# SSD core of a two-block model: the step of a state and what it gives to the next chunk as two steps of the written order

## The chip, the cores and the metric

The kernel runs on one core of a Trainium2 chip. The time is the device time of one execution in microseconds (us). Three runs of the kernel before gave 1649.72, 1649.62 and 1646.17 us, with a median of 1649.62 us.

## The reference

The program computes two blocks of a model on 512 tokens of width 1024. The first block has attention and an SSD mixer side by side and an MLP; the second has an RG-LRU layer and an MLA layer. The change lies in the SSD mixer alone, which works on 4 chunks of 128 tokens, forwards and backwards:

```python
def ssd_chunked(xdt, a, bm, cm):
    ...
    CB = jnp.einsum("bclgn,bcsgn->bgcls", Cc, Bc)
    M = CB[:, :, None] * jnp.exp(segsum(A))
    y_diag = jnp.einsum("bgrcls,bcsgrp->bclgrp", M, X)
    decay_states = jnp.exp(A_cs[..., -1:] - A_cs)
    states = jnp.einsum("bclgn,bgrcl,bclgrp->cbgrpn", Bc, decay_states, X)
    chunk_decay = jnp.moveaxis(jnp.exp(A_cs[..., -1]), -1, 0)
    ...
    def step(hs, inp):
        st, dec = inp
        return dec[..., None, None] * hs + st, hs
    ...
    _, prev = lax.scan(step, h0, (states, chunk_decay))
    y_off = jnp.einsum("bclgn,cbgrpn,bgrcl->bclgrp", Cc, prev, jnp.exp(A_cs))
    return (y_diag + y_off).reshape(b, s, h, p)
```

There are 4 groups of 8 heads. For each group a state is carried over the chunks in either direction, and what a chunk gets from the state of the chunk ahead of it is `y_off`. The inputs of this stage are an in-projection followed by a centred convolution of width 5 (x, B and C) and a gate z; behind it a product with `w_ssd_out` adds to the output.

## The kernel before

Large products are made of three: the activations are kept as a high and a low part (hi and lo), the weights too, and `hi*w_hi`, `lo*w_hi`, `hi*w_lo` are added up in PSUM (lines 174, 175 and 176). A block of one such product takes 24 matmuls of 128x512 here. A weight tile is loaded by a DMA of SP's queue into `wr`, cast to the high part `wh` on ScalarE (L162), and the low part `wl` is `wr - wh` (L165), in this stage on GpSimd (POOL) for two tiles of three and on VectorE (DVE) for the third. `wr`, `wh` and `wl` have four buffers each, so the cast of one weight tile waits until TensorE (PE) has done the last matmul with the `wh` four tiles earlier.

`ssd()` (L677) runs the 4 groups in turn. For each, the generator `ssd_core(g)` (L553) goes through the steps that are written in the string `CORE` (L41):

- **S n**, `state(n)`, n = 0 to 7, even numbers forwards and odd ones backwards, two for each chunk step (only 0 to 5 are needed): `xw` = x times decays on DVE (L596), a matmul with B into a PSUM tile (L598), and the state `st`: a copy on ScalarE for the first of either direction (L601), else `prev * decay` on DVE (L603) and the addition of the PSUM tile on DVE (L604). Then, in the same step, the matmul with C that gives the next chunk's share (L608), and its scaling into `yoff` on DVE (L615, or L612 and L613 where that chunk has been written by the other direction already).
- **M n**, `mixer(n)`, one of the 8 heads: two PE products that spread the cumulated decays (L623), for four chunks `e` (L629 ACT, L631 DVE) and `w` (L633 ACT, L635 DVE), the exponential (L642 ACT) and `e * w` on POOL (L643).
- **Y j**, `output(j)`, two heads each: 4 transposes of `yoff` (L650) and 8 matmuls with the `e` of the two heads (L653), the gate on DVE (L657, L659), a square on ACT (L665) that POOL adds up (L666), and the hi and lo part of the result (L669 ACT, L670 DVE).

Between the steps PE gets other blocks of 24 matmuls, called fills: the previous group's output product, the next group's x, B and C blocks with their convolution (`xbc`; x0 to x3 for x, x4 for B and x5 for C), and this group's gates (`z`, z0 to z3). When a fill is issued goes by its number and by NC (L42): after step number `step` all fills n with `n * NC <= (step + 1) * len(fill)` (L713). In the last group the fills are output products, gates and two steps of the attention's `qkv`.

A scheduler orders the instructions of each engine behind that by the times that it reckons with, so an engine's order is near to the written one but not the same. Each engine runs its instructions in its order: one that waits holds up all behind it.

Of the kernel before, what the change touches and what calls it, by code (L numbers as in the profile page):

```python
# [37 lines left out]
QG = 4  # L38
POM = 0
AORD = "s0 s1 s2 s3 f0 t0 m0 t1 m1 t2 m2 t3 m3 f1".split()  # L40
CORE = "S0 S1 M0 S2 S3 M1 S4 S5 M2 M3 Y0 M4 M5 Y1 M6 M7 Y2 Y3"  # L41
NC = 19  # L42
MODS = [0, 0, 6, 10]
WP = 0
TP = 0
# [14 lines left out]
class Build:  # L60
# [492 lines left out]
    def ssd_core(self, g):  # L553
# [20 lines left out]
        for i in range(2):  # L574
            x = self.t("cb", shape=(128, 4, 128))
# [4 lines left out]
        def hb(ap):  # L580
            return ap.unsqueeze(2).to_broadcast([128, 8, 64])

        def v8(ap):
            return ap.rearrange("p (h d) -> p h d", h=8)

        seen = set()
        prev = {}
        Ms = {}
        out = self.ssdT[g] = []

        def state(n):
            d = n % 2
            c = n // 2 if d == 0 else 3 - n // 2
            xw = self.t("xw")
            o = 32 * d + g * 8
            nc.vector.tensor_tensor(out=v8(xw), in0=v8(xtm[:, c]), in1=hb(self.tk2[:, c, o:o + 8]), op=ALU.mult)  # L596
            p = self.ps()
            nc.tensor.matmul(p, lhsT=Btm[:, c], rhs=xw, start=True, stop=True)  # L598
            st = self.t("st")
            if n < 2:  # L600
                nc.scalar.copy(out=st, in_=p)  # L601
            else:
                self.e("st").tensor_tensor(out=v8(st), in0=v8(prev[d]), in1=hb(self.dcy[:, c, o:o + 8]), op=ALU.mult)  # L603
                nc.vector.tensor_tensor(out=st, in0=st, in1=p, op=ALU.add)  # L604
            prev[d] = st
            cc = c + 1 if d == 0 else c - 1
            p = self.ps()
            nc.tensor.matmul(p, lhsT=CT[:, cc * 128:cc * 128 + 128], rhs=st, start=True, stop=True)  # L608
            eo = hb(self.tk2[:, cc, 64 + o:64 + o + 8])
            if cc in seen:  # L610
                y = self.t("yo")
                nc.vector.tensor_tensor(out=v8(y), in0=v8(p), in1=eo, op=ALU.mult)  # L612
                self.e("yo").tensor_tensor(out=yoff[:, cc], in0=yoff[:, cc], in1=y, op=ALU.add)  # L613
            else:
                nc.vector.tensor_tensor(out=v8(yoff[:, cc]), in0=v8(p), in1=eo, op=ALU.mult)  # L615
                seen.add(cc)
# [54 lines left out]
            out.append((hi, lo))  # L671

        for x in CORE.split():
            {"S": state, "M": mixer, "Y": output}[x[0]](int(x[1:]))
            yield

    def ssd(self, first):  # L677
# [19 lines left out]
        for g in range(4):  # L697
# [14 lines left out]
            for step, _ in enumerate(self.ssd_core(g)):  # L712
                while n < len(fill) and n * NC <= (step + 1) * len(fill):  # L713
                    with self.fills():
# [809 lines left out]
```

## Time and profile before

| | us |
|---|---|
| median of three runs | 1649.62 |
| profiled execution, device time | 1649.19 |
| its span, from the first to the last instruction | 1647.4 |
| PE busy in the span | 1580.8 |
| DVE busy | 1128.2 |
| ACT busy | 789.3 |
| POOL busy | 446.0 |
| the four groups of the SSD core, from us 100 to us 505 of the span | 405.00 |

The span is 1.8 us shorter than the execution's own time. The median of the runs is 0.4 us above that time. The stage that the change touches lies between us 100 and us 505: group 0 up to us 177, group 1 up to us 290, group 2 up to us 402, and group 3 behind it. The three later groups carry more fills than the first.

A line of the trace's timeline has the start in us, the length in us, the engine, the line of the kernel, and what is written and read; in square brackets stands how long the engine had been idle before, and what ended that. Consecutive matmuls overlap: the record of one is longer than the step to the next.

### The profile page before, as it was taken

To read this page: it belongs to the slowest core of one execution; us is meant where nothing else is said; L and a number is where in the kernel's file an instruction comes from. 1 tells how busy PE (TensorE), PEld (TensorE's weight loads), DVE (VectorE), ACT (ScalarE), POOL (GpSimd) and SP (SyncE) were. 2 spreads that over 40 slices of the span, in tenths; PEclk is the share of its full clock that TensorE was granted. 3 is DMA by queue.
4 is the path that set the end of the run, shared out by engine and by line. 5 is a ranking of instruction groups with operands and counts; after the bars stand their busy time and mean duration, and the time that the engine had idled before them with its cause. 6 is when DMAs were issued, how large, how long until landed. Compare 5 with 4: busy or idle time off the path is not lost.

```text
span 1647.4 us, 20884 instructions
## 1 busy us (share of the span) xinstructions
PE 1580.8 (96%) x7696; PEld 1279.2 (78%) x7696; DVE 1128.2 (68%) x1948; ACT 789.3 (48%) x1517; POOL 446.0 (27%) x322
## 2 busy tenths in 40 slices
PE   5989999999999999999999999999999999999998
PEld 3767667677688778778888888888888778988886
DVE  7899679689868988874445343443467884747883
ACT  4356546354465667663334232232336662454652
POOL 3314335244252443431133011111141011321012
PEclk8999999999999999999999999999999999999999
DMA  7612124224222222315313333323323222322211
GB/s 254 196 52 65 52 77 128 75 72 139 91 82 80 80 62 80 96 52 183 111 52 117 101 97 95 102 90 102 105 77 99 87 90 67 100 69 69 65 63 52
DMA packets 50649, 153.54 MB, mean 93 GB/s; under 512 B 8178, under 2 KB 12914, under 8 KB 50547
## 3 DMA queue, kind: packets, MB, share of 16 engines
q1 hardware_dynamic: 50546, 152.22, 28.9%
q8 instruction: 60, 0.98, 0.3%
q14 instruction: 43, 0.34, 0.1%
HBM read 150.10 MB, written 2.10 MB: 92 GB/s over the span
## 4 chain that ended last, share of the span: by engine, by line
PE 67%; DVE 18%; ACT 4%; issue 3%; POOL 3%; DMA 1%; DVEq 0%; POOLq 0%; ACTq 0%
PE pm L175 18%; PE pm L174 18%; PE pm L176 18%; DVE acc L507 3%; DVE wl L165 1%; DVE nmax L752 1%; PE px L608 1%; PE px L848 1%; DVE w L635 1%; PE px L598 1%; DMA wada<-in_w_ada 1%; POOL rs L254 1%; PE px L857 1%; POOL wl L165 1%; PE px L856 1%
## 5 line engine op out<-in xcount | busy, mean ns | idle before, releaser
L162 ACT CAST wh<-wr 128x1024 fp32r<-128x1024 f32 (+5 forms) x245 | 239.7, 980 | 389.3 <-PE pm L175 168.9
L165 DVE TENSOR_TENSOR wl<-wr,wh 128x1024 fp32r<-128x1024 f32 (+2 forms) x170 | 203.3, 1196 | 184.8 <-ACT wh L162 183.9
L165 POOL TENSOR_TENSOR wl<-wr,wh 128x1024 fp32r<-128x1024 f32 (+3 forms) x75 | 174.7, 2330 | 532.9 <-ACT wh L162 486.6
L174 PE MATMUL pm<-hh,wh 128*128 128x512 f32 x432 | 173.8, 406 | 8.2 <-ACT hh L169 6.6
L175 PE MATMUL pm<-hl,wh 128*128 128x512 f32 x432 | 176.0, 407 | 3.9 <-POOL hl L170 3.8
L176 PE MATMUL pm<-hh,wl 128*128 128x512 f32 x432 | 172.9, 401 | 0.0
L983 POOL TENSOR_TENSOR r<-r 128x512 f32<-128x512 f32 x32 | 50.8, 1589 | 252.3 <-ACT r L982 252.3
L174 PE MATMUL pm<-h,wh 128*128 128x512 f32 (+1 forms) x288 | 105.4, 366 | 0.0
L175 PE MATMUL pm<-h,wh 128*128 128x512 f32 (+1 forms) x288 | 105.3, 365 | 0.0
L176 PE MATMUL pm<-h,wl 128*128 128x512 f32 (+1 forms) x288 | 105.2, 365 | 0.0
L174 PEld LDWEIGHTS pm<-hh,wh 128*128 128x128 f32 x432 | 81.8, 190 | 29.9 <-ACT hh L169 8.4
L175 PEld LDWEIGHTS pm<-hl,wh 128*128 128x128 f32 x432 | 82.3, 190 | 27.1 <-POOL hl L170 7.6
L174 PE MATMUL pm<-wh,rh 128*128 128x512 f32 x256 | 99.8, 390 | 0.0
L760 POOL TENSOR_SCALAR pr<-pr,psum 128x512 f32<-128x512 f32 x64 | 64.8, 1024 | 128.8 <-DVE psum L756 71.6
L176 PE MATMUL pm<-wh,rl 128*128 128x512 f32 x256 | 99.6, 389 | 0.0
L175 PE MATMUL pm<-wl,rh 128*128 128x512 f32 x256 | 99.6, 389 | 0.0
L176 PEld LDWEIGHTS pm<-hh,wl 128*128 128x128 f32 x432 | 82.4, 191 | 19.9 <-issue 3.1
L507 DVE SCALAR_TENSOR_TENSOR acc<-pm,conv_w_s,acc 128x510 f32<-128x510 f32 (+2 forms) x118 | 87.4, 741 | 8.3 <-ACT acc L498 7.3
L279 DVE SCALAR_TENSOR_TENSOR wada<-wada,cs 128x1024 f32<-128x1024 f32 x48 | 68.9, 1446 | 16.4 <-DMA wada<-in_w_ada 15.8
L643 POOL TENSOR_TENSOR e<-e,w 128x512 f32<-128x512 f32 x32 | 52.0, 1626 | 101.1 <-ACT e L642 87.0
L755 ACT ACTIVATE pr<-px,nmax 128x512 f32<-128x512 f32 (+2 forms) x96 | 60.5, 638 | 29.8 <-DVE nmax L752 23.9
L174 PE MATMUL pm<-ha,wh 128*128 128x512 f32 (+1 forms) x192 | 68.2, 355 | 0.0
(401 smaller groups left out, 4120.3 us busy)
## 6 DMA issues: line engine op xcount, KB each, us to landing
wr<-in_w_mlp SPq DMA_DIRECT2D x64, 512.0 KB, 3.5
wada<-in_w_ada SPq DMA_DIRECT2D x48, 512.0 KB, 4.0
wr<-in_w_xbc SPq DMA_DIRECT2D x24, 512.0 KB, 3.5
wr<-in_w_in_a SPq DMA_DIRECT2D x20, 512.0 KB, 3.5
wr<-in_w_z SPq DMA_DIRECT2D x16, 512.0 KB, 3.6
wr<-in_w_ssd_out SPq DMA_DIRECT2D x16, 512.0 KB, 3.6
wr<-in_w_gate SPq DMA_DIRECT2D x16, 512.0 KB, 3.7
wr<-in_w_qkv SPq DMA_DIRECT2D x16, 384.0 KB, 3.0
```

The source lines that it names most:

```text
L162: nc.scalar.copy(out=hi[:, :n], in_=raw[:, :n])
L165: eng.tensor_tensor(out=lo[:, :n], in0=raw[:, :n], in1=r32(hi[:, :n]), op=ALU.subtract)
L174: m(out, lhsT=lh, rhs=rh, start=start, stop=False)
L175: m(out, lhsT=lh, rhs=rl, start=False, stop=False)
L176: m(out, lhsT=ll, rhs=rh, start=False, stop=stop)
L254: g.tensor_tensor(out=r, in0=r, in1=self.mhalf.to_broadcast(list(ss.shape)) if len(ss.shape) == 2 else self.mhalf.unsqueeze(2).to_broadcas ...
L279: nc.vector.scalar_tensor_tensor(out=w, in0=w, scalar=1.0, in1=self.cs, op0=ALU.mult, op1=ALU.mult, accum_out=self.modc[:, j:j + 1])
L507: nc.vector.scalar_tensor_tensor(out=acc[:, lo:hi], in0=ps[:, lo + o:hi + o], scalar=w[:, j:j + 1], in1=acc[:, lo:hi], op0=ALU.mult, op1=A ...
L643: self.e("ew").tensor_tensor(out=e, in0=e, in1=w, op=ALU.mult)
L755: nc.scalar.activation(out=e[:, :n], in_=p, func=AF.Exp, bias=nmax, accum_out=s)
L760: self.e("norm").tensor_scalar(out=e[:, :n], in0=e[:, :n], scalar1=s, scalar2=1.0, op0=ALU.mult, op1=ALU.mult)
L983: self.e("sq").tensor_tensor(out=r, in0=r, in1=r, op=ALU.mult)
```

## The change

The step of a state is cut behind the state itself: `state(n)` ends with `st` and puts it into `held`, and a new step **C n**, `carry(n)`, takes it from there, does the matmul with C and scales the result into `yoff`. The string `CORE` places the six new steps, one step or more behind their states, and the number of steps NC by which the fills are spread goes from 19 to 25. The computation is the same.

```diff
--- before.py
+++ after.py
@@ -38,8 +38,8 @@
 QG = 4
 POM = 0
 AORD = "s0 s1 s2 s3 f0 t0 m0 t1 m1 t2 m2 t3 m3 f1".split()
-CORE = "S0 S1 M0 S2 S3 M1 S4 S5 M2 M3 Y0 M4 M5 Y1 M6 M7 Y2 Y3"
-NC = 19
+CORE = "S0 S1 C0 M0 C1 S2 S3 M1 C2 C3 S4 S5 M2 C4 C5 M3 Y0 M4 M5 Y1 M6 M7 Y2 Y3"
+NC = 25
 MODS = [0, 0, 6, 10]
 WP = 0
 TP = 0
@@ -584,7 +584,7 @@
             return ap.rearrange("p (h d) -> p h d", h=8)
 
         seen = set()
-        prev = {}
+        prev, held = {}, {}
         Ms = {}
         out = self.ssdT[g] = []
 
@@ -603,6 +603,14 @@
                 self.e("st").tensor_tensor(out=v8(st), in0=v8(prev[d]), in1=hb(self.dcy[:, c, o:o + 8]), op=ALU.mult)
                 nc.vector.tensor_tensor(out=st, in0=st, in1=p, op=ALU.add)
             prev[d] = st
+            held[n] = st
+
+        def carry(n):
+
+            d = n % 2
+            c = n // 2 if d == 0 else 3 - n // 2
+            o = 32 * d + g * 8
+            st = held.pop(n)
             cc = c + 1 if d == 0 else c - 1
             p = self.ps()
             nc.tensor.matmul(p, lhsT=CT[:, cc * 128:cc * 128 + 128], rhs=st, start=True, stop=True)
@@ -671,7 +679,7 @@
             out.append((hi, lo))
 
         for x in CORE.split():
-            {"S": state, "M": mixer, "Y": output}[x[0]](int(x[1:]))
+            {"S": state, "C": carry, "M": mixer, "Y": output}[x[0]](int(x[1:]))
             yield
 
     def ssd(self, first):
```

Each engine has as many instructions as before and of the same kinds. The lines of the code behind the cut have numbers that are 8 higher in the changed kernel: the matmul with C is L616 there, the scaling L623 (L620, L621), `mixer`'s matmuls L631, its exponential L650, `e * w` on POOL L651, and `output`'s matmuls L658 and L661. The order of the instructions differs in the SSD stage and the first bit of the attention behind it, and nowhere else; behind that the two kernels' orders are the same on all engines. On SP's queue only loads of group 3 have changed places: two gates' weights and modulation weights with tables of the attention.

**PE, group 1, states 4 and 5.** Names are tiles: `px` PSUM of the small products, `xw` and `st` as above, `pm` a fill's PSUM tile, `pf` and `pg` the mixer's. Before, the states' matmuls stood so:

```order
L598 MATMUL px318_1801<-xw317_1799,Btm254_1482 128x512
L175 MATMUL pm325_1819<-hl4_103,wh327_1821 128x512
L176 MATMUL pm325_1819<-hh3_102,wl328_1822 128x512
L174 MATMUL pm325_1819<-hh3_102,wh327_1821 128x512
L175 MATMUL pm325_1819<-hl4_103,wh327_1821 128x512
L176 MATMUL pm325_1819<-hh3_102,wl328_1822 128x512
L608 MATMUL px320_1806<-st319_1803,th144_890 128x512
L598 MATMUL px322_1811<-xw321_1809,Btm254_1482 128x512
```

Now the two L598 stand one behind the other,

```order
L175 MATMUL pm317_1799<-hl4_103,wh319_1801 128x512
L176 MATMUL pm317_1799<-hh3_102,wl320_1802 128x512
L598 MATMUL px324_1841<-xw323_1839,Btm254_1482 128x512
L598 MATMUL px327_1848<-xw326_1846,Btm254_1482 128x512
L174 MATMUL pm329_1853<-hh3_102,wh331_1855 128x512
L175 MATMUL pm329_1853<-hl4_103,wh331_1855 128x512
```

and their carries (L616, with `st325` and `st328`) a block later:

```order
L175 MATMUL pm329_1853<-hl4_103,wh331_1855 128x512
L176 MATMUL pm329_1853<-hh3_102,wl332_1856 128x512
L631 MATMUL pf334_1887<-csb_585,sel_552 128x512
L631 MATMUL pg335_1888<-csb_585,sel_552 128x512
L616 MATMUL px338_1911<-st325_1843,th143_887 128x512
L174 MATMUL pm339_1914<-hh3_102,wh341_1916 128x512
```

Between `st325`'s L598 and its L616 now stand the other L598, the 24 matmuls of one block and the two of a mixer; before, between `st319`'s L598 and its L608 stood five, and four between those of the state that follows. The second carry follows 24 matmuls behind the first. In group 2 the distances are the same; in groups 0 and 3 a carry has fewer matmuls ahead of it.

**ACT and POOL, group 0, the fourth head (M3).** On ACT before, with `e189` the fourth head's exponents, `th200` of a convolution, `zt213` of a gate and `wh270` a weight cast:

```order
L629 ACTIVATE e189_1097<-pg188_1094,tk1_586 128x128
L633 ACTIVATE w190_1098<-cb120_774,tk1_586 128x128
L515 ACTIVATE th200_1175<-acc199_1169 128x512
L533 ACTIVATE zt213_1257<-pm209_1226 128x512
L642 ACTIVATE e189_1097<-e189_1097 128x512
L162 CAST wh270_1543<-wr269_1542 128x1024
L662 ACTIVATE ssacc_589<-yd192_1130 128x512
```

and now, with `e195` for the same head and `wh269` for the same weight:

```order
L637 ACTIVATE e195_1137<-pg194_1134,tk1_586 128x128
L641 ACTIVATE w196_1138<-cb120_774,tk1_586 128x128
L515 ACTIVATE th191_1127<-acc190_1121 128x512
L162 CAST wh269_1540<-wr268_1539 128x1024
L650 ACTIVATE e195_1137<-e195_1137 128x512
L533 ACTIVATE zt205_1209<-pm201_1178 128x512
```

The cast has gone ahead of the exponential of the fourth head. On POOL before (`wl241` is the low part of the weights of block x3, the other `wl` those of other blocks; `e137`, `e162`, `e180`, `e189` are heads 0 to 3):

```order
L165 TENSOR_TENSOR wl212_1229<-wr210_1227,wh211_1228 128x1024
L643 TENSOR_TENSOR e137_833<-e137_833,w138_834 128x512
L165 TENSOR_TENSOR wl241_1397<-wr239_1395,wh240_1396 128x1024
L643 TENSOR_TENSOR e162_955<-e162_955,w163_956 128x512
L165 TENSOR_TENSOR wl258_1491<-wr256_1489,wh257_1490 128x1024
L643 TENSOR_TENSOR e180_1039<-e180_1039,w181_1040 128x512
L643 TENSOR_TENSOR e189_1097<-e189_1097,w190_1098 128x512
```

and now (`wl236` is block x3's, `e136`, `e158`, `e183`, `e195` heads 0 to 3):

```order
L165 TENSOR_TENSOR wl204_1181<-wr202_1179,wh203_1180 128x1024
L651 TENSOR_TENSOR e136_830<-e136_830,w137_831 128x512
L651 TENSOR_TENSOR e158_945<-e158_945,w159_946 128x512
L651 TENSOR_TENSOR e183_1067<-e183_1067,w184_1068 128x512
L651 TENSOR_TENSOR e195_1137<-e195_1137,w196_1138 128x512
L165 TENSOR_TENSOR wl236_1374<-wr234_1372,wh235_1373 128x1024
L165 TENSOR_TENSOR wl258_1491<-wr256_1489,wh257_1490 128x1024
```

The low part of block x3's weights stood behind head 0 and now stands behind head 3. `wh269` takes the buffer of `wh203`, which PE reads last in the last two matmuls of block z3. From the second last of these to the first matmul that reads `wl236` there are ten on PE: two of block z3, two of M4, two of block x2, one of M5, two of block x3 and the other of M5.

**ACT, group 1, the last head (M7).** Before, `e390` is that head, `wh436` and `wh446` are weight casts, `acc396` is the convolution of a block:

```order
L629 ACTIVATE e390_2211<-pg389_2208,tk1_586 128x128
L633 ACTIVATE w391_2212<-cb263_1530,tk1_586 128x128
L162 CAST wh436_2446<-wr435_2445 128x1024
L642 ACTIVATE e390_2211<-e390_2211 128x512
L498 ACTIVATE acc396_2262<-pm392_2231,conv_b_s_538,conv_w_s_536 128x512
L162 CAST wh446_2492<-wr445_2491 128x1024
L665 ACTIVATE sq400_2287<-yd399_2284 128x512
```

and now `e396` is the last head, `wh456` the weight cast, `acc407` the convolution of block x3:

```order
L641 ACTIVATE w397_2252<-cb263_1530,tk1_586 128x128
L637 ACTIVATE e396_2251<-pg395_2248,tk1_586 128x128
L641 ACTIVATE w397_2252<-cb263_1530,tk1_586 128x128
L162 CAST wh456_2553<-wr455_2552 128x1024
L515 ACTIVATE th393_2244<-acc392_2238 128x512
L498 ACTIVATE acc407_2325<-pm403_2294,conv_b_s_538,conv_w_s_536 128x512
L650 ACTIVATE e396_2251<-e396_2251 128x512
L673 ACTIVATE sq400_2287<-yd399_2284 128x512
```

The exponential of the last head now stands behind a weight cast and behind the first step of block x3's convolution; before, only the earlier cast `wh436` stood ahead of it. `wh456` waits for the second last matmul of block x3, and POOL makes its low part ahead of `e396 * w`.

## Rows read from the trace of the kernel before

**Rows 1.** Page, part 1, busy time of each engine.

```profile
PE 1580.8 (96%) x7696; PEld 1279.2 (78%) x7696; DVE 1128.2 (68%) x1948; ACT 789.3 (48%) x1517; POOL 446.0 (27%) x322
```

**Rows 2.** Windows, us 100 to 505: busy time of each engine, sum of four windows.

```profile
sum 405.00, PE 388.48 PEld 290.21 DVE 336.20 ACT 213.46 POOL 159.06; mean PE 97.12 PEld 72.55 DVE 84.05 ACT 53.36 POOL 39.76
```

**Rows 3.** Waits of PE, us 100 to 520: total us, times, longest.

```profile
PE px L608 <- DVE st L604: 6.9, 5, 2.5
PE px L598 <- DVE xw L596: 2.7, 2, 1.5
PE pm L175 <- DVE yl L670: 2.0, 2, 1.8
PE px L561 <- DVE th L516: 1.7, 1, 1.7
PE pm L174 <- DVE acc L507: 1.7, 1, 1.7
PE px L653 <- POOL e L643: 1.2, 1, 1.2
```

**Rows 4.** Timeline of DVE, us 217.5 to 223.8.

```profile
218.45 2.87 DVE L603 TENSOR_TENSOR st<-st,dcy 128x512 f32<-128x512 f32 x1
221.24 1.75 DVE L596 TENSOR_TENSOR xw<-xtm,tk 128x512 f32<-128x512 f32 x1
222.91 0.68 DVE L604 TENSOR_TENSOR st<-st,px 128x512 f32<-128x512 f32 x1
```

**Rows 5.** Timeline of POOL, us 217 to 224.

```profile
217.84 2.93 POOL L165 TENSOR_TENSOR wl<-wr,wh 128x1024 fp32r<-128x1024 f32 x1 [4.21 <-ACT wh L162]
220.73 1.71 POOL L643 TENSOR_TENSOR e<-e,w 128x512 f32<-128x512 f32 x1
```

**Rows 6.** Single lines, us 100 to 510: duration min/median/max in ns, first and last start.

```profile
L603 DVE TENSOR_TENSOR st<-st,dcy x16: 677/686/2866, 119.7 to 439.4; 128x512 f32<-128x512 f32 x16
L604 DVE TENSOR_TENSOR st<-st,px x16: 672/680/689, 121.2 to 442.4; 128x512 f32<-128x512 f32 x16
```

**Rows 7.** Timeline of PE, us 222.5 to 228.5.

```profile
223.64 1.35 PE L608 MATMUL px<-st,th 128*128 128x512 f32 x2 [2.48 <-DVE st L604]
...
227.78 0.42 PE L174 MATMUL pm<-hh,wh 128*128 128x512 f32 x1
```

**Rows 8.** Windows: length, busy time (instructions) of PE, PEld, DVE, ACT, POOL, then PE's granted clock.

```profile
224.00:226.00 2.00, 2.00 (x5) 0.86 (x3) 0.88 (x2) 0.00 (x0) 0.00 (x0) 0.60 0.00 0
226.00:228.00 2.00, 2.00 (x5) 1.22 (x4) 0.69 (x1) 0.00 (x0) 0.00 (x0) 0.55 0.00 0
...
336.00:340.00 4.00, 2.16 (x7) 1.07 (x7) 3.22 (x6) 0.00 (x0) 0.14 (x1) 1.00 0.28 107
```

**Rows 9.** Timeline of PE, two matmuls of one block at us 206 in group 1.

```profile
206.01 0.40 PE L175 MATMUL pm<-hl,wh 128*128 128x512 f32 x1
206.25 0.39 PE L176 MATMUL pm<-hh,wl 128*128 128x512 f32 x1
```

**Rows 10.** Single lines of ACT and POOL, us 100 to 510, min/median/max in ns.

```profile
L162 ACT CAST wh<-wr x49: 822/1046/1085, 105.0 to 506.1; 128x1024 fp32r<-128x1024 f32 x43, 128x768 fp32r<-128x768 f32 x6
L642 ACT ACTIVATE e<-e x32: 614/632/672, 119.6 to 489.1; 128x512 f32<-128x512 f32 x32
L643 POOL TENSOR_TENSOR e<-e,w x32: 1270/1507/2843, 120.3 to 489.8; 128x512 f32<-128x512 f32 x32
L165 POOL TENSOR_TENSOR wl<-wr,wh x31: 1828/2406/3559, 106.1 to 481.6; 128x1024 fp32r<-128x1024 f32 x28, 128x768 fp32r<-128x768 f32 x3
```

**Rows 11.** Timeline of POOL, us 125 to 152 (end of group 0's fourth head).

```profile
136.07 2.84 POOL L165 TENSOR_TENSOR wl<-wr,wh 128x1024 fp32r<-128x1024 f32 x1
...
147.65 2.32 POOL L643 TENSOR_TENSOR e<-e,w 128x512 f32<-128x512 f32 x1 [1.89 <-DVE yd L657]
```

**Rows 12.** Timeline of ACT, us 270 to 279 (end of group 1).

```profile
273.84 0.81 ACT L498 ACTIVATE acc<-pm,conv_b_s,conv_w_s 128x512 f32<-128x512 f32 x1
```

**Rows 13.** Timeline of PE, us 281 to 287 (transposes behind group 1).

```profile
282.91 1.53 PE L561 MATMUL px<-ident,th 128*128 128x128 f32 x12
```

## The prediction

> **What bounds the kernel now.** I read the page first: PE is busy for 96% of the span, DVE for 68% [rows 1]. So only what PE stands idle for can be won, and only in the stage whose order changes. The windows of that stage give it: of 405.0 us PE is busy for 388.5, so 16.5 us are idle, while DVE has work for 336 and POOL for 159 [rows 2]. PE's list of waits then says for whom [rows 3]. The longest entry is the matmul with C (L608) that waits five times for the state's addition (L604), 6.9 us in all; the matmul with B waits twice for `xw`, 2.7 us; four more entries make 6.6 us. DVE and POOL bound nothing by their sums; they matter where PE waits for a single instruction of theirs.
>
> Why is the state late? Normally the addition follows its PSUM tile at once. In the longest of the five cases DVE was at `prev * decay` (L603) for 2.87 us, then at `xw` for 1.75 us, and only then came the addition [rows 4]. Just then POOL ran a weight remainder for 2.93 us and `e * w` for 1.71 us [rows 5]. L603 takes 0.69 us in the median and up to 2.87; L604, which reads one of its inputs from PSUM, never takes more than 0.69 [rows 6]. So DVE's instructions with both inputs in SBUF were held while POOL worked, and the waits of L608 are such collisions, not a lack of DVE time.
>
> **What the waits of L608 cost, and what of it goes.** The record of a matmul lasts 0.40 us but the next starts 0.23 us later [rows 9], so a gap costs 0.16 us more than the idle time shown: 6.9 + 5 x 0.16 = 7.7 us. Behind the longest gap, of 2.48 us, the granted clock was 0.60 and 0.55 in the two windows that follow [rows 8]; the 4.14 us from L608 to the matmul at us 227.78 [rows 7] held work for about 4.14 x 0.58 = 2.4 us, so 1.7 us more. Behind the gap of 1.84 us at us 336 to 338 the clock stayed 1.00 [rows 8]. Together 9.4 us hang on these five waits. They lie in groups 1 and 2, where the new order puts a whole block between the additions and the matmuls that read them: 24 x 0.23 = 5.5 us. The late state of rows 4 was late by about 2.5 us. I take all of it as gone: **-9.4 us**; bounds -9.4 and, if the states are late by more than a block, -5.
>
> By the Trainium skill, page "SBUF — State Buffer", section "Who interferes with whom", a DVE instruction with two SBUF inputs and a GpSimd instruction that reads SBUF shut each other out for a whole instruction instead of sharing. The trace agrees in L603's 2.87 us beside the remainder's 2.93. The rule speaks against the change: the same DVE and POOL instructions are still there, so the split takes no collision away and only alters which instruction is hit and who waits for it.
>
> **The matmul with B.** In the new order two of these (L598) stand one behind the other, with the two `xw` ahead of them. Its waits were 2.7 + 2 x 0.16 = 3.0 us [rows 3]. Nothing removes their cause. I put 0; bounds -3.0 (gone) and +2 (one more such gap of 1.5 us and a margin).
>
> **Group 0, block x3: a new wait.** ACT now has the weight cast ahead of the fourth head's exponential, and POOL has block x3's remainder behind that head's `e * w`. Before, this remainder was made at us 136.07, 11 us ahead of that multiplication at us 147.65 [rows 11]. The cast waits for the second last matmul of block z3. From that matmul's start: 0.40 for it, 1.05 cast, 0.63 exponential, 1.51 `e * w`, 2.41 remainder [rows 10], 6.0 us. PE has ten matmuls to do meanwhile, 10 x 0.23 = 2.3 us. It then waits **3.7 us**; with the minima of rows 10 it is 4.9 - 2.3 = 2.6, with the maxima 8.5 - 2.3 = 6.2. All of these are above the 2.48 us that halved the clock, so I add the 1.7 us of above: **+5.4 us**, bounds 2.6 and 8.
>
> **Ends of the groups.** The last output step needs the last head. Group 1: before, the exponential stood ahead of a convolution's first step. Now it is behind it and behind a cast, and on POOL `e * w` is behind that cast's remainder: from the second last matmul of block x3, 0.40 + 1.05 + 2.41 + 1.51 = 5.4 us. PE has ten matmuls (2.3 us) and ten small ones meanwhile, eight of them transposes, at 1.53 / 12 = 0.13 us each [rows 13], 3.6 us together. **+1.8 us**; bounds 0.7 by the minima and 4.3 by the maxima. Group 2: the exponential is likewise behind block x3's first convolution step, 0.8 us [rows 12], with no remainder between: **+0.5**, bounds 0.3 and 1. Group 3: the last head's `e * w` stands behind other POOL work, and only four matmuls (0.9 us) lie between the last carry and the transposes that read it, whose scaling on DVE alone is some 0.7 as L604's is [rows 6]: **+1.0**, bounds 0 and 2.3, one remainder. Group 0: the 1.2 us that L653 waited for `e` [rows 3] falls to some 0.4, since PE comes later there: **-0.9**, bounds -1.4 and 0.
>
> **The rest at nothing.** NC only moves fills, and every engine's instructions are the same in number and kind. The scaling into `yoff` waits for a later matmul; a block or a mixer's work lies between it and the transposes that read it, except in group 3, priced above. SP's exchanged loads: no entry of PE's waits names a load [rows 3]; one would cost at most what that list's longest does, 2.5 us. The waits for `yl`, `th` and `acc` (5.4 us) have no part in the cut and stay.
>
> **Sum.** -9.4 + 5.4 + 1.8 + 0.5 + 1.0 - 0.9 = -1.6 us. The profiled execution took 1649.19 us (span 1647.4 and 1.8 around it), so 1647.6; the median of the runs, 1649.62, lies 0.4 above it. A measurement of this kernel tells about 0.3% (4.9 us) from nothing: faster is below 1644.7, slower above 1654.6.
>
> **Rivals.**
> *R1, faster: the new waits stay small.* The order of POOL holds, but its work there runs at the minima, and no gap lowers the clock. Then -9.4 - 0.9 + 2.6 (x3) + 0.7 (group 1) + 0.3 (group 2), and L598's 3.0 us go as well since both `xw` stand ahead: -9.7, **1639.5 us**; without the last, 1642.5. For it: L643's minimum and median are close (1.27 and 1.51). Against it: the ten matmuls of cover are too few at any duration in rows 10. Chance 0.27.
>
> *R2, slower: POOL's collisions now hit the chains that PE waits for.* The cast, remainder, `e * w` chain at block x3 and at the end of group 1 has two POOL steps that stretch to 3.56 and 2.84 us [rows 10]. Then x3 costs 6.2 + 1.7, group 1 4.3 + 1.7, groups 2 and 3 1 and 2.3: with -9.4 and 0 for the end of group 0, +7.8, **1657 us**. It decides where a chain outlasts PE's cover by over about 2 us, for between 1.84 and 2.48 us the clock begins to fall. For it: PE waited five times for a late state before, and both chains now hold two POOL steps. Against it: the medians of rows 10 lie nearer the minima than the maxima. Chance 0.18.
>
> *R3, the change doesn't do what it says: the late instruction is another.* The held DVE instruction is then `xw`, a convolution's product or a scaling, with PE behind it. If half of the 9.4 us comes back so, -4.7 + 5.4 + 1.8 + 0.6 = +3.1: **1652.3 us**; if all, 1657. For it: the number of collisions is as before. Against it: the entries for `xw`, `th` and `acc` in rows 3, which are exposed before too, make 6.1 us in four waits beside L608's 6.9. Chance 0.10.
>
> By the page's rule R3 would be the rule and not the exception; a block's cover is what makes me hold it small.
>
> **How the numbers follow.** My forecast, 1647.6 with bounds of some 3 us to either side, has 0.45; nearly all of it lies within 0.3%. R1 is faster but for its upper end, R2 slower, R3 within but for its upper end. So faster 0.30 (R1 and a little of the forecast), same 0.46, slower 0.24. The range reaches from R1's 1640 to 1655.5, near R2, and leaves out about 0.1 at either end; the forecast's own is 1644.5 to 1651.
>
> **What would show it.** PE's list of waits: no L616 with `st` (right), a wait of the third product L176 for `wl` on POOL of 3 to 4 us near us 145 to 155 with a granted clock near 0.5 behind it, L661 with `e` at the end of group 1 near 2 us, and L598 with `xw` twice, as before. The windows of the four groups give the sum: 402 to 405 us in place of 405. I am wrong if L616 still waits for `st`, if the wait for `wl` is below 1 us (R1), if the ends of the groups cost more than 5 us (R2), or if another DVE instruction takes L604's place at the top of the list (R3).

## The result and the profile after

The changed kernel took 1661.53 us (median of six runs, 1659.05 to 1669.29) beside 1649.13 us for the kernel before: 1.0083 times as long, with an interval of 1.0071 to 1.0095. It is slower by 12.4 us in the median. The forecast was 1647.6 us with a range up to 1655.5, so the time lies above the range. The span of the profiled execution went from 1647.4 to 1660.5 us, 13.1 us longer.

First PE's list of waits of the changed kernel, us 100 to 520, as in [rows 3] (total us, times, longest):

```profile
PE pm L176 <- POOL wl L165: 4.3, 1, 4.3
PE pm L175 <- DVE yl L678: 4.0, 2, 3.9
PE px L661 <- POOL e L651: 3.8, 3, 2.1
PE px L598 <- DVE xw L596: 3.7, 4, 1.5
PE px L658 <- ACT e L637: 3.2, 2, 1.7
PE pm L174 <- DVE acc L507: 1.7, 1, 1.7
PE pm L174 <- DVE accS L551: 0.9, 1, 0.9
```

The 6.9 us of the matmul with C are gone: L616 is in no row. In its place stand four waits that were small or absent, and the one for `th` (1.7 us) is gone too. The seven rows sum to 21.6 us, against 16.2 in [rows 3]: 5.4 us more. That is less than half of what was lost. The rest shows in the windows of the changed kernel around those waits (columns as in [rows 8]; the last three are granted clock, DMA share, GB/s):

```profile
152.00:156.00 4.00, 3.40 (x9) 2.69 (x10) 4.00 (x6) 0.49 (x2) 3.31 (x2) 0.57 0.61 196
288.00:296.00 8.00, 8.00 (x33) 5.82 (x32) 8.00 (x12) 4.71 (x8) 3.02 (x2) 0.57 0.21 74
394.00:402.00 8.00, 8.00 (x31) 5.78 (x30) 7.57 (x15) 3.73 (x9) 3.78 (x2) 0.57 0.18 54
500.00:504.00 4.00, 2.91 (x8) 2.34 (x8) 4.00 (x14) 1.11 (x4) 0.40 (x1) 0.57 0.00 0
558.00:562.00 4.00, 4.00 (x13) 3.29 (x14) 2.40 (x5) 1.05 (x2) 3.65 (x2) 0.57 0.41 133
```

A mean of 0.57 in each: most of these 28 us ran at the 1.2 GHz level. What the full clock would have saved is the length times 1 - 0.57: 1.7 + 3.4 + 3.4 + 1.7 + 1.7 = 12 us. Before, there was one such stretch from us 104 on, at us 224 to 228 [rows 8], 1.7 us. So by this working the clock costs 10 us more than before. That is a little too much: by the two pages PE's busy time went from 1580.8 to 1589.2 us for the same 7696 matmuls and its idle time from 66.6 to 71.3 us, 8.4 and 4.7 us of the 13.1. In part of the stretches PE waits anyway, and the small matmuls of an output step do not take twice as long at half clock: from L658 to L661 it is 0.72 us at us 288.85 and 0.42 us at us 288.06, just before the clock fell.

What stands ahead of each stretch? In the timelines of the changed kernel, ACT, POOL and PE at the fourth head of group 0:

```profile
146.31 1.05 ACT L162 CAST wh<-wr 128x1024 fp32r<-128x1024 f32 x1 [3.04 <-PE pm L175]
147.27 0.63 ACT L650 ACTIVATE e<-e 128x512 f32<-128x512 f32 x1
...
147.98 1.28 POOL L651 TENSOR_TENSOR e<-e,w 128x512 f32<-128x512 f32 x1 [7.97 <-ACT e L650]
149.22 6.09 POOL L165 TENSOR_TENSOR wl<-wr,wh 128x1024 fp32r<-128x1024 f32 x2
...
152.60 1.22 PE L176 MATMUL pm<-hh,wl 128*128 128x512 f32 x2 [4.26 <-POOL wl L165]
```

This is the chain of the prediction, step for step: the cast waits for PE, the exponential for the cast, POOL's multiplication for that, and the remainder of block x3 is last. It is the first of the two remainders in the POOL row; alone it took 3.33 us, where the prediction had put the median of 2.41, while DVE made a remainder of its own and a `yl` that took 2.83 us (us 150.26). At the end of group 1:

```profile
281.89 1.05 ACT L162 CAST wh<-wr 128x1024 fp32r<-128x1024 f32 x1 [2.47 <-PE pm L175]
...
284.04 0.62 ACT L650 ACTIVATE e<-e 128x512 f32<-128x512 f32 x1
...
283.02 2.40 POOL L165 TENSOR_TENSOR wl<-wr,wh 128x1024 fp32r<-128x1024 f32 x1 [3.88 <-ACT wh L162]
...
283.50 2.46 DVE L516 SCALAR_TENSOR_TENSOR th<-th,acc 128x512 f32<-128x512 f32 x1 [1.60 <-ACT th L515]
285.89 0.34 DVE L643 SCALAR_TENSOR_TENSOR w<-cb,tk,w 128x128 f32<-128x128 f32 x1
...
286.37 1.27 POOL L651 TENSOR_TENSOR e<-e,w 128x512 f32<-128x512 f32 x1 [0.95 <-DVE w L643]
...
287.69 0.43 PE L661 MATMUL px<-e,xtm 128*64 128x128 f32 x2 [2.14 <-POOL e L651]
```

This is the predicted order, but its last link is another. POOL had done its remainder and stood idle for 0.95 us, since the last `w` of the head (L643) came late on DVE. Ahead of that `w` stood a convolution's product (L516), which took 2.46 us beside POOL's remainder of 2.40 us; its median in this stage is 0.69 us. So the 2.1 us are in part a collision on DVE.

Two things were not in the prediction. One is a wait of the third output step for a PSUM tile, since ACT had not yet read a head's `pg` (groups 1 and 2):

```profile
275.68 0.49 PE L658 MATMUL px<-ident,yoff 128*128 128x128 f32 x2 [1.73 <-ACT e L637]
...
392.77 0.49 PE L658 MATMUL px<-ident,yoff 128*128 128x128 f32 x2 [1.51 <-ACT e L637]
```

The other is in group 3, where the low part of an output (`yl`, L678) stood on DVE behind a step of the attention that waited for POOL. It stood so before too, so first the kernel before and then the changed one:

```profile
495.45 2.38 DVE L797 TENSOR_TENSOR qkv<-qkv,rs 128x320 f32<-128x320 f32 x3 [3.44 <-POOL rs L254]
497.76 0.74 DVE L670 SCALAR_TENSOR_TENSOR yl<-yd,ssd_norm_w_s,yh 128x512 fp32r<-128x512 f32 x1
```

```profile
498.02 2.35 DVE L805 TENSOR_TENSOR qkv<-qkv,rs 128x320 f32<-128x320 f32 x3 [3.44 <-POOL rs L254]
500.30 0.74 DVE L678 SCALAR_TENSOR_TENSOR yl<-yd,ssd_norm_w_s,yh 128x512 fp32r<-128x512 f32 x1
...
501.09 0.80 PE L175 MATMUL pm<-yl,wh 128*128 128x512 f32 x1 [3.86 <-DVE yl L678]
```

DVE waits equally long, 3.44 us, in both. But before it was the third output's `yl`, and PE had the fourth output step to do meanwhile and waited 1.85 us. Now the attention's fill comes earlier, the `yl` is the second output's, and the last two heads and output steps lie behind the wait.

### The profile page after: what moved, and what is told of

It is laid out like the page before. It is cut to its first block, busy times and chain, and to the rows that moved or that the text cites. A ratio compares the mean times of both kernels' runs of the same rounds, so it can differ in the third digit from the quotient of the medians.

```text
span 1660.5 us, 20904 instructions
## 1 busy us (share of the span) xinstructions
PE 1589.2 (96%) x7696; PEld 1286.2 (77%) x7696; DVE 1135.9 (68%) x1948; ACT 789.9 (48%) x1517; POOL 433.9 (26%) x322
## 4 chain that ended last, share of the span: by engine, by line
PE 70%; DVE 16%; ACT 4%; issue 3%; POOL 3%; DMA 0%; POOLq 0%; DVEq 0%; ACTq 0%
PE pm L175 19%; PE pm L174 19%; PE pm L176 19%; DVE acc L507 2%; DVE wl L165 1%; DVE nmax L760 1%; PE px L856 1%; PE px L598 1%; PE px L661 1%; PE px L658 1%; PE px L616 1%; POOL rs L254 1%; DVE w L643 1%; PE px L865 1%; PE px L864 1%
## 5 line engine op out<-in xcount | busy, mean ns | idle before, releaser
L165 POOL TENSOR_TENSOR wl<-wr,wh 128x1024 fp32r<-128x1024 f32 (+3 forms) x75 | 170.7, 2278 | 528.3 <-ACT wh L162 470.8
L174 PE MATMUL pm<-hh,wh 128*128 128x512 f32 x432 | 178.0, 416 | 8.3 <-ACT hh L169 6.6
L507 DVE SCALAR_TENSOR_TENSOR acc<-pm,conv_w_s,acc 128x510 f32<-128x510 f32 (+2 forms) x118 | 87.4, 740 | 11.7 <-ACT acc L498 10.9
L651 POOL TENSOR_TENSOR e<-e,w 128x512 f32<-128x512 f32 x32 | 47.4, 1482 | 118.5 <-ACT e L650 112.8
```

Of the source, the lines that this page charges most:

```text
L165: eng.tensor_tensor(out=lo[:, :n], in0=raw[:, :n], in1=r32(hi[:, :n]), op=ALU.subtract)
L174: m(out, lhsT=lh, rhs=rh, start=start, stop=False)
L507: nc.vector.scalar_tensor_tensor(out=acc[:, lo:hi], in0=ps[:, lo + o:hi + o], scalar=w[:, j:j + 1], in1=acc[:, lo:hi], op0=ALU.mult, op1=A ...
L651: self.e("ew").tensor_tensor(out=e, in0=e, in1=w, op=ALU.mult)
```

## The experiments

The change does two things that its diff shows as one: it cuts the states, and with a longer string and NC = 25 it issues the fills at other steps. By the rule of L713 the fills behind M3 come a step or two earlier. Groups 1 and 2 have 14 fills, groups 0 and 3 have ten. In group 1, for example, with fills in brackets (the output product's four come earlier):

```
before   M3 [x0] Y0 M4 [z2] M5 [x1] Y1 [z3] M6 M7 [x2] Y2 [x3] Y3
changed  M3 [z2] Y0 [x1] M4 M5 [z3] Y1 M6 [x2] M7 Y2 [x3] Y3
```

Two theories were put against each other. **Theory P**: the places of the fills cost the time, and the cut gains. **Theory C**: the cut itself gives the new order and its waits. In the kernels below `CUM` or `AT` replaces the rule of L713 by a table of how many fills have been issued after each step. Each was timed beside the kernel before.

### split_oldfill: the cut, with the fills behind the same steps as before

```diff
-NC = 25
+NC = 19; AT = [0, 1, 2, 2, 3, 3, 4, 5, 6, 6, 6, 7, 8, 9, 9, 9, 10, 11, 12, 13, 14, 15, 16, 17, 18]
...
-                while n < len(fill) and n * NC <= (step + 1) * len(fill):
+                while n < len(fill) and n * NC <= (AT[step] + 1) * len(fill):
```

> The states are cut as in the change and the carries stand at its places, but each fill is issued behind the same S, M or Y step as in the kernel before. Theory P (the places of the fills, which NC = 25 and the longer string move, set the new waits; the cut itself takes L608's waits away): no wait of L176 for wl, no half clock near the ends of groups 1 and 2, no wait of the matmul with C for st, 1640 to 1644 us, ratio to before 0.994 to 0.997. Rival C (the cut itself makes the scheduler's new order and the waits): 1655 to 1662 us, ratio 1.004 to 1.008, with the waits for wl and for the last head's e still there.

1651.7 us, ratio 1.0017 (1.0009 to 1.0026). The 10 us of the fills' places are gone, but the cut gains nothing; it costs 3 us. PE's list of waits of this kernel, first rows, and then DVE and POOL ahead of state 4 of group 1:

```profile
PE px L598 <- DVE xw L596: 10.1, 6, 2.0
PE px L661 <- POOL e L651: 2.9, 2, 1.7
```

```profile
221.99 3.49 DVE L621 TENSOR_TENSOR yoff<-yoff,yo 128x512 f32<-128x512 f32 x2
225.41 0.68 DVE L596 TENSOR_TENSOR xw<-xtm,tk 128x512 f32<-128x512 f32 x1
...
220.82 2.41 POOL L165 TENSOR_TENSOR wl<-wr,wh 128x1024 fp32r<-128x1024 f32 x1 [4.25 <-ACT wh L162]
223.18 1.75 POOL L651 TENSOR_TENSOR e<-e,w 128x512 f32<-128x512 f32 x1
```

No matmul with C waits for a state, but the matmul with B now waits six times for `xw`, 10.1 us, which were 2.7 [rows 3]. The late carries put their scaling into `yoff` on DVE just ahead of the next states' `xw`. Two additions with both inputs in SBUF took 3.49 us there while POOL worked, in place of about 1.3, and `xw` came behind them. The six are not all of this kind: in two of them `xw` itself took 2.34 and 2.33 us beside a remainder (us 198.01 and 308.36), and ahead of the one at us 411.77, in group 3, no held instruction stands. Neither theory expected this; it is what R3 of the prediction describes: the collisions stayed and another matmul waits.

### nosplit_newfill: the fills at the change's places, the states uncut

```diff
-NC = 19
+NC = 25; AT = [0, 1, 3, 5, 6, 7, 10, 11, 12, 15, 16, 17, 18, 19, 20, 21, 22, 23, 24]
```

> The kernel before, state in one step, but each fill is issued behind the same S, M or Y step as in the changed kernel. Theory P: L608's waits stay in kind (some 5 to 9 us) and the waits at the ends of groups 1 and 2 with their half clock come (12 us), 1656 to 1662 us, ratio 1.004 to 1.008. Rival C: the ends are as in the kernel before, 1647 to 1652 us, ratio 0.998 to 1.002. Both expect no long wait for wl of block x3 in group 0 if that one needs cut and fills together.

1663.4 us, ratio 1.0076 (1.0052 to 1.010). Theory P holds, if a little above its range: with the fills alone the kernel loses as much as with the whole change. The wait for `wl` of block x3 is not there, as both expected; it needs cut and fills together.

### before_tail_new and tail_old: only the fills from M3 on

`before_tail_new` is the kernel before with the change's fills from M3 on; `tail_old` is the changed kernel with the old ones there. Group 1's table in either:

```diff
 before_tail_new
-while n < len(fill) and n * NC <= (step + 1) * len(fill):
+while n < len(fill) and n < CUM[g][step]:
...
 tail_old, steps M3 Y0 M4 M5 Y1 M6 M7 Y2 Y3
-10 11 11 12 12 13 13 14 14
+9 9 10 11 12 12 13 14 14
```

> The kernel before, with its uncut states, and only the fills from M3 on at the places of the change. Theory T: 1657 to 1664 us, ratio 1.005 to 1.009, with the waits for the last head's e, for ACT's e ahead of an output and 3.9 us for yl, and half clock near them. Rival F: 1647 to 1652 us.

> The changed kernel, with the fills from M3 on at the places that they have in the kernel before, and those ahead of M3 at the change's. Theory T (the fills behind M3, which the change issues a step or two earlier and which then lack at the outputs, cost the time): no wait of L658 for ACT, no wait over 1.8 us at the ends, no half clock there, 1645 to 1652 us, ratio to before 0.998 to 1.002. Rival F (the fills ahead of M3 cost it): 1658 us or more, ratio above 1.005.

`before_tail_new`: 1674.29 us, ratio 1.0149 (1.0127 to 1.0172). `tail_old`: 1648.86 us, ratio 0.9999 (0.9986 to 1.0012). So with the fills from M3 on at their old places the changed kernel loses nothing, and those ahead of M3 cost it nothing. Not every sign of theory T came true in `tail_old`: PE waits 3.0 us for a convolution behind group 2 (1.7 in [rows 3]), and in the profiled execution (1653.75 us) half clock near us 150, 180 and 503 costs 6.8 us. The loss in the uncut kernel is larger than expected (25 us and not 8 to 15). PE's waits and the two longest stretches of `before_tail_new` show both parts again:

```profile
PE px L608 <- DVE st L604: 7.5, 6, 2.5
PE px L650 <- ACT e L629: 6.1, 2, 3.3
PE pm L175 <- DVE yl L670: 4.0, 2, 3.9
PE px L653 <- POOL e L643: 3.6, 4, 2.1
```

```profile
280.00:288.00 8.00, 8.00 (x32) 5.43 (x33) 5.69 (x16) 3.22 (x10) 1.27 (x1) 0.57 0.22 68
...
508.00:530.00 22.00, 19.62 (x72) 12.74 (x73) 13.65 (x32) 6.49 (x15) 4.64 (x5) 0.53 0.00 1
```

The wait for `yl` is 3.9 us as in the changed kernel, but the stretch behind it is 22 us long and not 4: it alone costs 22 x 0.47 = 10 us.

What is the cut worth by itself? That is read from kernels whose fills are all at the same places:

| | states uncut | states cut |
|---|---|---|
| all fills at the old places | 1649 | 1651.7 (`split_oldfill`) |
| all fills at the new places | 1663.4 (`nosplit_newfill`) | 1661.5 (the change) |

With the old places the cut costs 3 us, and with the new ones the intervals overlap. `before_tail_new` and the changed kernel differ also in the fills ahead of M3 (in groups 1 and 2 block x0 is issued ahead of M3 by the change and behind it in `before_tail_new`), so their 13 us are not the cut's. Nor are those fills always free: beside the new ones from M3 on, the uncut kernel is 11 us faster with the new places ahead of M3 (`nosplit_newfill`) than with the old; PE's waits are 18.6 us there and 27.3 us in `before_tail_new`.

### g12_old and g3_old: which groups

The changed kernel with the old fills from M3 on in groups 1 and 2 alone, and in group 3 alone (the same tables as `tail_old`, the other groups left as changed).

> The changed kernel with the fills of groups 1 and 2 alone, from M3 on, at the old places. If the waits of L658 for ACT (3.2 us), of L661 for e (2.7 us there) and the two half-clock stretches behind them (6.7 us lost) come from those fills: none of them, 1649 to 1653 us (ratio 1.000 to 1.003). If they come from the cut: 1659 to 1662 us.

> The changed kernel with the fills of group 3 alone, from M3 on, at the old places. If the 3.9 us wait for yl near us 500, its half clock and what the attention behind it loses are the work of those fills: yl waits 1.9 us as before, no half clock near us 500, 1654 to 1658 us (ratio 1.003 to 1.006). If group 3 has no part in it: 1660 to 1662 us.

`g12_old`: 1656.91 us, ratio 1.0046 (1.003 to 1.0062): 4.6 us less than the changed kernel, where 8 to 12 were expected. `g3_old`: 1655.84 us, ratio 1.0046 (1.0032 to 1.0059): 5.7 us less, as expected. In `g12_old` the waits for ACT's `e` and L661's at these ends are gone as expected, but PE waits there for a convolution in their place, with 1.7 us of half clock behind it at us 400; in `g3_old` the wait for `yl` is back at 1.8 us. Against the expectation half clock follows that wait too (1.7 us, us 504 to 510), where the kernel before had kept its clock. First `g12_old`, then `g3_old`, from PE's waits:

```profile
PE px L561 <- DVE th L516: 3.1, 2, 1.9
...
PE px L658 <- DVE yoff L623: 1.2, 2, 0.8
PE px L661 <- POOL e L651: 1.1, 1, 1.1
```

```profile
PE px L658 <- ACT e L637: 3.5, 2, 2.0
PE pm L175 <- DVE yl L678: 1.8, 1, 1.8
```

The attention's wait near us 558 (2.2 us, and half clock behind it) is back at 0.9 us in `g3_old`, as in the kernel before, and stays at 2.3 us in `g12_old`, so it hung on group 3's fills too. The parts do not add up: 4.6 + 5.7 leaves 2.4 of `tail_old`'s 12.7 us for group 0, where block x3's wait and its half clock alone are 6.0 us.

### x3_rem_dve and late_mul_dve: one queue place on POOL each

```diff
 x3_rem_dve
+        self.rem = (g, i) == (1, 3); self.gemm_cm([[self.a["w_xbc"][m]]], self.h, evac); self.rem = 0
...
-        eng = nc.gpsimd if (self.lo_n * self.lo_pool) % 12 < self.lo_pool else nc.vector
+        eng = nc.vector if getattr(self, 'rem', 0) else nc.gpsimd if (self.lo_n * self.lo_pool) % 12 < self.lo_pool else nc.vector
 late_mul_dve
-            self.e("ew").tensor_tensor(out=e, in0=e, in1=w, op=ALU.mult)
+            (nc.vector if n == 7 and g < 3 else self.e("ew")).tensor_tensor(out=e, in0=e, in1=w, op=ALU.mult)
```

> The changed kernel, with the low part of block x3's weights (the block issued in group 0) made on DVE in place of POOL. If that one queue place on POOL costs what the trace shows, 4.3 us of waiting and 1.7 us of half clock behind it, the time falls from 1661.5 to about 1655.5 us, ratio to before 1.004 to 1.005. Rival: PE only waits for something else at that place (the yh of the output, another remainder), 1659 to 1662 us.

> The changed kernel, with e * w of the last head of groups 0 to 2 on DVE in place of POOL, so that it no longer stands behind a weight remainder. The waits of L661 for e (2.1 us in group 1, 0.6 in group 2) should go. If the half clock at the end of group 1 (3.3 us lost) follows from the 2.1 us wait, it goes too and the time is about 1656 us, ratio 1.004; the half clock at the end of group 2 stays, since there a wait of 1.5 us for ACT stands ahead of it. Rival: the half clock comes from the earlier wait for ACT or from the small matmuls of the output steps, then it stays and the time is 1658.5 to 1660 us.

`x3_rem_dve`: 1658.52 us, ratio 1.0068 (1.0046 to 1.009). The 4.3 us wait and its half clock are gone, but PE now waits 2.1 us for DVE at two mixers' matmuls (L631, 0.5 and 1.6 us); 3 us of the 6 expected are gained by the medians, between theory and rival; the interval overlaps the changed kernel's, so even these are not sure. `late_mul_dve`: 1661.48 us, ratio 1.0078 (1.0066 to 1.0091), so nothing gained. L661's waits went and so did the half clock behind them. But in this kernel the stretch came earlier, behind the wait for ACT at us 275.83, where the changed kernel had kept its clock (first `late_mul_dve`, then the changed kernel):

```profile
275.83 0.49 PE L658 MATMUL px<-ident,yoff 128*128 128x128 f32 x2 [1.51 <-ACT e L637]
...
276.00:284.00 8.00, 8.00 (x33) 5.43 (x34) 6.06 (x17) 3.56 (x11) 1.27 (x1) 0.57 0.22 69
288.00:296.00 8.00, 6.85 (x39) 4.66 (x39) 8.00 (x12) 2.81 (x5) 2.67 (x2) 1.00 0.41 130
```

```profile
276.00:284.00 8.00, 8.00 (x49) 5.82 (x48) 6.40 (x18) 5.51 (x13) 2.25 (x2) 1.00 0.21 69
```

So the expectation's two-way choice was too simple: a gap of 1.5 us was followed by half clock in one kernel, and one of 1.73 us at the same place was not in the other. At the end of group 2 the 1.5 us wait for ACT was still there and the clock stayed 1.00 (us 394 to 402), against the expectation.

### xw_first, xw_tail_old, xw_earlier and before_xw: the xw of a state early

If the cut only moved the wait from `st` to `xw`, then `xw`, which needs nothing of the carries, should be made ahead of them. `scaled(n)`, step **X n**, is L596 alone; `state(n)` takes its tile.

```diff
+        def scaled(n, xw=None):
+            ...
+            nc.vector.tensor_tensor(out=v8(xw), in0=v8(xtm[:, c]), in1=hb(self.tk2[:, c, o:o + 8]), op=ALU.mult)
...
-CORE = "S0 S1 C0 M0 C1 S2 S3 M1 C2 C3 S4 S5 M2 C4 C5 M3 Y0 M4 M5 Y1 M6 M7 Y2 Y3"
+CORE = "S0 S1 X2 X3 C0 M0 C1 S2 S3 M1 X4 X5 C2 C3 S4 S5 M2 C4 C5 M3 Y0 M4 M5 Y1 M6 M7 Y2 Y3"   xw_first, xw_tail_old
+CORE = "S0 S1 X2 X3 C0 M0 C1 S2 S3 X4 X5 M1 C2 C3 S4 S5 M2 C4 C5 M3 Y0 M4 M5 Y1 M6 M7 Y2 Y3"   xw_earlier
+CORE = "S0 S1 X2 X3 M0 S2 S3 X4 X5 M1 S4 S5 M2 M3 Y0 M4 M5 Y1 M6 M7 Y2 Y3"   before_xw
```

> The run split_oldfill (states cut, fills at the old places, 1651.7 us) with xw of states 2 to 5 as a step of its own, ahead of the carries of the two states before: S0 S1 X2 X3 C0 M0 C1 S2 S3 M1 X4 X5 C2 C3 S4 S5 and so on. Theory X (the cut kept the collisions and moved the wait from st to xw, which now stands on DVE behind the scaling into yoff): L598's 10.1 us of waiting fall below 3 us and no wait for st returns, 1642 to 1646 us, ratio 0.995 to 0.998. Rival M (whatever stands next on DVE is late in its turn, PE waits as long elsewhere): 1649 to 1653 us, ratio 1.000 to 1.003.

> The same early xw in the kernel of the run tail_old (fills ahead of M3 at the change's places, behind it at the old ones). Theory X: 1640 to 1645 us, ratio 0.994 to 0.998. Rival M: as tail_old, 1647 to 1652 us.

`xw_first` (fills as before): 1645.96 us, ratio 0.9976 (0.9966 to 0.9987), faster than the kernel before, by 3.5 us where 3 to 7 were expected: L598's waits fell from 10.1 to 5.2 us, not below 3. `xw_tail_old` (fills of the change ahead of M3): 1648.19 us, ratio 0.9995 (0.9983 to 1.0006), no gain that can be told.

> The run xw_first (1646.0 us) with xw of states 4 and 5 one mixer earlier, right behind S3. In xw_first L598 still waited for xw 1.4 and 2.1 us at state 4 of groups 1 and 2, when POOL held that xw. If the place of xw decides: these two waits go, 1641 to 1645 us, ratio 0.994 to 0.997. If POOL then holds whatever DVE does at that time and PE waits for that: 1645 to 1649 us.

`xw_earlier`: 1639.12 us, ratio 0.9942 (0.9929 to 0.9955), 9.4 us faster than the kernel before and better than expected. Its whole list of PE's waits:

```profile
PE px L665 <- POOL e L655: 2.8, 2, 1.5
PE pm L176 <- DVE wl L165: 2.4, 1, 2.4
PE pm L175 <- DVE yl L682: 1.8, 1, 1.8
PE pm L174 <- DVE acc L507: 1.7, 1, 1.7
PE px L602 <- DVE xw L593: 1.3, 1, 1.3
PE pm L174 <- ACT yh L681: 0.9, 1, 0.9
```

10.9 us in place of 16.2, with none for a state and one for `xw` (L602 is L598 here). And no window of two us between us 104 and 520 has a lowered clock.

> The kernel before, with its uncut states and its fills, and only xw of states 2 to 5 made early, as in the run xw_earlier (1639.1 us). If the early xw alone is what that run gained: L608 then waits for st only while prev * decay is held, some 3 to 4 us in place of 6.9, and the time is 1639 to 1645 us, ratio 0.994 to 0.998. If early xw and cut are needed together: the waits for st stay at 5 us or more and the time is 1646 to 1650 us.

`before_xw`: 1648.69 us, ratio 0.9995 (0.9986 to 1.0004). The early `xw` alone does nothing: there the uncut L608 (L612 in it) waits nine times for `st`, 9.6 us. Beside the old fills, cut and early `xw` are needed together; cut alone is `split_oldfill`.

## Why the prediction was wrong

- **What L608's waits cost, and that they go from the matmul with C.** Right in the changed kernel: L616 waits for no state, the half clock at us 224 is gone, and L598's waits grew by 1.0 us, inside the bound of +2. But this gain is not the cut's own. With the fills left as they were, L598's waits grow from 2.7 to 10.1 us (`split_oldfill`) and the cut gains nothing: the 0 for L598 held by where the fills stood, which the prediction did not weigh. The scaling into `yoff` was priced for whoever waits for it and not for what it now stands ahead of. "The waits of L608 are such collisions" also read too much into the longest: three of the five, 5.5 us, lie behind a held DVE instruction, and ahead of the two at us 201 and 314 (0.3 and 1.1 us) none was held. The rule of the page "SBUF — State Buffer" of the Trainium skill, cited against the change, held: beside POOL's work DVE's L516 took 2.46 us in the changed kernel, and two additions into `yoff` 3.49 us in `split_oldfill`.
- **Block x3 in group 0.** Right in mechanism and nearly in size: 4.3 us of waiting against 3.7, half clock worth 1.7 us behind it, as forecast. The remainder ran 0.9 us above the median that was put for it.
- **Ends of groups 1 and 2.** L661's waits were 2.1 and 0.6 us against 1.8 and 0.5: right in number, and in group 1 partly by luck, for there the last link was DVE's `w` behind a held convolution and not POOL's remainder. At the end of group 0 it waits 1.1 us, 1.2 before, so the -0.9 was wrong. What failed is the price of what follows. I put no clock on them since a gap of 1.84 us had left the clock alone [rows 8]; here each group's end lost 3.4 us to it. And I missed L658's wait for ACT, 3.2 us: I followed POOL's order to the last head's `e * w`, and not the PSUM tiles that ACT has to read before the output step can have one.
- **Group 3.** +1.0 was the worst term. Neither the last head nor the last carry is waited for; it is 3.9 us for `yl`, against 1.8 before [rows 3], half clock, and a wait in the attention behind it. `g3_old` puts it at 5.7 us. "The waits for yl, th and acc have no part in the cut and stay" was wrong for `yl`: the attention's step, which waits 3.44 us for POOL before and after, now stands ahead of the second output's `yl` and not the third's. It was wrong for `th` too, whose wait went; that for `acc` stayed.
- **"NC only moves fills", at nothing.** This is the step that failed and decided the case. The instructions are the same, but their places alone cost the uncut kernel 15 us (`nosplit_newfill`), and with the fills from M3 on put back the changed kernel takes 1648.9 us (`tail_old`). Of the rivals R2 had the right sign and the right mechanism (chains outlasting PE's cover at block x3 and at the ends, the clock falling), at 1657 us and a chance of 0.18; it took POOL's stretched work as the reason. That was so for block x3's remainder (3.33 us), while at the end of group 1 POOL ran near its medians (2.40, 1.27 us) and DVE was held; the waits for ACT and for `yl`, where the cover was too thin, it did not have.

What is shown and what is not: that the places of the fills from M3 on are the cause is shown by `tail_old`, which undoes them in the changed kernel, and by `before_tail_new`, which brings them into the uncut one. How the 13 us divide between idle time and clock is read from rows of one execution each, and the clock's part differs between kernels (stretches of 4 us and 22 us behind the same wait). What decides whether and how long the clock falls behind a gap of 1.5 us or more is left open.

## What to carry to other kernels

When steps are added to a schedule that spreads other work by the number of steps, count what the new steps do to the spread: here the steps with next to no PE work took places in the first half, and the last mixers and outputs, where the waits then stood, got less. When an instruction is moved off a critical place because a neighbour holds it, look at what it then stands ahead of; the gain came only when the next instruction in line, `xw`, was moved too, and only beside the old fills (`xw_earlier`; `xw_tail_old` gained nothing). A wait of 1.5 us on a busy PE is to be priced with the half clock that may follow, not at 1.5 us.

## What was unexpected of the hardware

Gaps of PE that differed little were followed by very different clocks. Behind 1.84 us [rows 8] and, at us 275.68 of the changed kernel, 1.73 us the clock stayed 1.00; behind 1.51 us at us 392.77 of the same run it was at half for some 7 us. So R2's "between 1.84 and 2.48 us the clock begins to fall" does not hold. Behind the 3.86 us wait for `yl` it was at half for some 3.4 us in the changed kernel and for about 20 in `before_tail_new`. The kind of work right behind the gap does not sort them: an output step with its small matmuls stood behind the gaps at us 275.68, 287.69 and 392.77 alike, and in `g3_old` a stretch of some 7 us (us 150 to 158, mean 0.57) held 128x512 matmuls alone. What does was not tried.
